# A hybrid DeltaNet/gMLP layer on one core: gate rows loaded earlier, o scaled and turned in another order, and a last tile that ends in fewer steps

## The chip, the core and the metric

The kernel runs on one core of one Trainium2 chip. The metric is device time in microseconds (us) of one execution, as the median of several runs. A profiled execution gives a trace: every instruction with its engine, its line in the kernel, its start and length.

The engines are TensorE (PE; its weight loads are listed as PEld), VectorE (DVE), ScalarE (ACT), GpSimd (POOL) and SyncE (SP), which here only issues DMAs. Each engine works through its own instructions in order, so an instruction that waits holds up everything behind it on its engine.

## The reference

One layer of a diffusion backbone, on 128 context tokens (`x_prompt`) and 2048 latent tokens (`x_sample`), model width 1024:

```python
h = modulated rmsnorm(x)                       # shift, scale, gate from c or, for the context, c_ctx
proj = h @ w_in                                # q, k, v, gate, a/b, u, vg
o_a = gated DeltaNet, forward + backward scan, 4 heads x 128, chunks of 64
o_a = rmsnorm(o_a, o_norm) * silu(gate)
o_b = gelu(u) * (w_spatial @ layernorm(gelu(vg)) + b_spatial)
x = x + gate1 * (concat(o_a, o_b) @ w_out)
h = modulated rmsnorm(x)
x = x + gate2 * (relu(h @ w_ff1) ** 2 @ w_ff2)
y = rmsnorm(x, norm_final)
```

The scan solves, for each chunk of 64 tokens, a triangular system and carries a 128 x 128 state per head from chunk to chunk. The outputs are y for both sequences and the context's two final states.

## The kernel before, in words

The 2176 tokens are 17 tiles of 128 (tile 0 is the context), `NT = 17`. The program has three stages: the head (modulation, input projections and convolution), the scan, and the MLP.

**Scan.** A unit is one tile in one direction: two units for the context, 16 forward, 16 backward. The triangular systems of two units are solved together (a pair), by doubling: `level(w)` for w = 2, 4, 8, 16, 32 makes a product into PSUM (L1173), DVE copies it under a mask into a kept matrix, P2 to P32 in this text (L1176, `copy_predicated`), and PE then takes P as an operand (L1187 and L1193). So at each level PE needs a DVE instruction that needs PE. The rest of a unit is `prep` (KK, QK: L1026, L1036), `values` and `scan` (vt L1054, S L1085, o L1108).

**Output steps.** For the context and in the backward scan, `o_steps` finishes a tile. `norm` loads ob (the gMLP half), squares o on ACT and makes 1/rms per head with a power on POOL. `scaled` multiplies that factor (L1398) and then, head by head, o by it and by the gate (four instructions at L1400). `trans(half)` turns half 0 (o) or half 1 (ob) on PE (L1413), makes a high part on ACT (oH, L1417) and a low part on DVE (oL, L1418), and, in half 0, asks for the two halves of x (L1409). `proj(n, k0)` multiplies with w_out: four steps for each of two column halves n, in groups of three matmuls, `mm3` (L220 high x high, L221, L222 with the low parts). Its last step multiplies the PSUM sum by the gate row (L1437, `tmp`), adds x (L1438) and stores (L1440). For the latent tiles the gate rows, `ga1`, are loaded once. For the context tile each row is loaded there, by `wrow` (L213), into one of the 49 buffers of 128 x 512 that `wp` has for weights, rows and activations alike; a load into such a buffer is issued by SP once the earlier user has let go.

**Order.** Each step goes into a list with a time, in units of the scan: `at(time, step, kind)`; `spread` puts a list of steps evenly in a span. `o_steps` gives its first four steps parts 0 to 1 of a window (`p3[4]` to `p3[5]`; for the context 0.4 units from `NT + 0.9`). The list is sorted by time and emitted. A scheduler then orders the instructions of each engine by a timeline of its own, so that a step moved in the list also moves others.

**MLP.** Seven Strassen-like products go over pairs of latent tiles; `todo` is the list of (product, pair, quarter). `outcome` adds a product's PSUM sum into accumulators. When a tile is whole, `final` makes its end: times the gate row, plus x, squares with a sum, 1/rms over both halves (`rsqrt_cols`: DVE at L177, POOL's power at L178), times 1/rms and norm_final (L1879), stores (L1880). `half_out` does one half; the other half is done as soon as its sum is there. The last entry of `todo` is the last sum of the last tile, with accumulator y[0].

Of the kernel before, what the change touches and what calls it, by code (L numbers as in the profile page):

```python
# [8 lines left out]
F32 = mybir.dt.float32  # L9
# [4 lines left out]
AF = mybir.ActivationFunctionType  # L14
ALU = mybir.AluOpType
# [3 lines left out]
P = 128  # L19
D = 1024  # L20
KT = D // P
# [3 lines left out]
H = 4  # L25
EPS = 1e-6
# [36 lines left out]
def hybrid_step(  # L63
# [7 lines left out]
    V, A, G, T = nc.vector, nc.scalar, nc.gpsimd, nc.tensor  # L71
    load = nc.sync.dma_start
    store = nc.sync.dma_start
# [4 lines left out]
    def yrow(t):  # L78
        return y_prompt[0] if t == 0 else y_sample[0, (t - 1) * P : t * P, :]

    def cond(t):
        return 0 if t == 0 else 1
# [9 lines left out]
    mod_d = dp.tile([2, 6 * D], F32, name="mod_d")  # L92
# [117 lines left out]
    def wrow(row):  # L210

        t = w512("row")
        load(out=t, in_=row.to_broadcast([P, 512]))  # L213
        return t
# [66 lines left out]
    with ExitStack() as ph:  # L281
# [103 lines left out]
        ps = pt()  # L385
# [541 lines left out]
    with ExitStack() as ph:  # L927
# [448 lines left out]
        def o_steps(du):  # L1376
            t = du["t"]
            out = []
            u = {}

            def norm():
                du["ob"] = w512("ob")
                load(out=du["ob"], in_=ob_d[t * P : (t + 1) * P, :])
                o, ga = du["o"], du["ga"]
                ss = smp.tile([P, 4], F32, tag="oss", name="oss")
                junk = fp.tile([P, P], BF16, tag="junk", name="junk", bufs=1)
                for h in range(H):
                    A.activation(junk, o[:, h, :], AF.Square, accum_out=ss[:, h : h + 1])
                r2 = smp.tile([P, 4], F32, tag="r2", name="r2")
                rr = smp.tile([P, 4], F32, tag="rr", name="rr")  # L1390
                V.tensor_tensor(out=r2, in0=rq[:, t, :], in1=rq[:, t, :], op=ALU.mult)
                V.tensor_tensor(out=r2, in0=r2, in1=ss, op=ALU.mult)
                rsqrt_cols(rr, r2, 4, 1.0 / P, EPS)
                u["rr"] = rr

            def scaled():
                o, ga, rr = du["o"], du["ga"], u["rr"]
                V.scalar_tensor_tensor(out=rr, in0=rr, scalar=0.5, in1=rq[:, t, :], op0=ALU.mult, op1=ALU.mult)  # L1398
                for h in range(H):
                    V.scalar_tensor_tensor(out=o[:, h, :], in0=o[:, h, :], scalar=rr[:, h : h + 1],  # L1400
                                           in1=ga[:, h * P : (h + 1) * P], op0=ALU.mult, op1=ALU.mult)

            def trans(half):
                def f():
                    if half == 0:
                        u["H"], u["L"] = [], []
                        u["x"] = [w512("x"), w512("x")]
                        for n in range(2):
                            load(out=u["x"][n], in_=xrow(t)[:, n * 512 : (n + 1) * 512])  # L1409
                    src = du["o"] if half == 0 else du["ob"].rearrange("p (h d) -> p h d", h=H)  # L1410
                    ps = pj().rearrange("p (h d) -> p h d", h=H)
                    for h in reversed(range(H)):
                        T.transpose(ps[:, h, :], src[:, h, :], ident)  # L1413
                    hs = hp.tile([P, 4, P], F32R, tag="h", name="oH")
                    ls = hp.tile([P, 4, P], F32R, tag="h", name="oL")
                    scale = 0.5 if half else vec[:, 68:69]
                    A.activation(hs, ps, AF.Copy, scale=scale)  # L1417
                    V.scalar_tensor_tensor(out=ls, in0=ps, scalar=scale, in1=f32(hs), op0=ALU.mult, op1=ALU.subtract)  # L1418
                    u["H"] += [hs[:, i, :] for i in range(4)]
                    u["L"] += [ls[:, i, :] for i in range(4)]  # L1420
                return f

            def proj(n, k0):
                def f():
                    if k0 == 0:
                        u["ps"] = pj()
                    for k in (k0, k0 + 1):
                        mm3(u["ps"], [(u["H"][k], u["L"][k]) + WO[n][k]], first=k == 0,
                            last=k == KT - 1)
                    if k0 == KT - 2:  # L1430
                        sl = slice(n * 512, (n + 1) * 512)
                        tmp = fp.tile([P, 512], F32, tag="ug" if n else "vg", name="tmp")
                        ga = ga1[n]
                        if cond(t) == 0:
                            ga = wrow(mod_d[0:1, 2 * D + n * 512 : 2 * D + n * 512 + 512])
                        x = u["x"][n]
                        V.tensor_tensor(out=tmp, in0=u["ps"], in1=ga, op=ALU.mult)  # L1437
                        V.tensor_tensor(out=x, in0=x, in1=tmp, op=ALU.add)  # L1438
                        du["x2"] = u["x"]
                        store(out=x2_d[t * P : (t + 1) * P, sl], in_=x)  # L1440
                return f

            for n in range(2):
                for k0 in range(0, KT, 2):
                    out.append(proj(n, k0))
            return [(0.0, norm, "fill"), (0.45, scaled, None), (0.7, trans(0), "fill"), (0.95, trans(1), "fill")], out

        def swap_right():
            right.close()
# [143 lines left out]
    def add(out, a, b, op=ALU.add):  # L1593
        V.tensor_tensor(out=out, in0=a, in1=b, op=op)  # L1594
# [158 lines left out]
    y0 = {}  # L1753
# [23 lines left out]
    def fetch(src, name="r2"):  # L1777
        t = w512(name)
        load(out=t, in_=src)
        return t  # L1780
# [79 lines left out]
    def half_out(y, n, x, ga, ss):  # L1860

        add(y[n], y[n], ga[n], ALU.mult)
        add(y[n], y[n], x[n])
        A.activation(x[n], y[n], AF.Square, accum_out=ss[:, n : n + 1])

    def final(t, y):

        ga = gate_rows(0) if t == 0 else rows["ga"]
        x = [fetch(x2_d[t * P : (t + 1) * P, n * 512 : n * 512 + 512], "x") for n in range(2)]
        ss = smp.tile([P, 2], F32, tag="ss2", name="ss2")  # L1870
        half_out(y, 1, x, ga, ss)

        def rest():
            half_out(y, 0, x, ga, ss)
            r = smp.tile([P, 1], F32, tag="r", name="r")
            add(ss[:, 0:1], ss[:, 0:1], ss[:, 1:2])
            rsqrt_cols(r, ss[:, 0:1], 1, 1.0 / D, EPS)
            for n in range(2):
                V.scalar_tensor_tensor(out=y[n], in0=y[n], scalar=r, in1=rows["nf"][n], op0=ALU.mult, op1=ALU.mult)  # L1879
                store(out=yrow(t)[:, n * 512 : n * 512 + 512], in_=y[n])  # L1880

        return rest
# [134 lines left out]
    for m, (n, i, u, q) in enumerate(todo):  # L2017
        us = products[n][1]
        s_next(m + AHEAD + 2, True)
        s_next(m + AHEAD, False)  # L2020
        if n == 5 and u == 0 and q == 0:
            rows["ga"] = gate_rows(1)
            rows["nf"] = row512(norm_final.unsqueeze(0))
        if q == 0:
            ps = bank()
            if i == 4:
                rest = final(pairs[u][1], [acc["v", u], acc["q", u]])
            elif i == 2:
                rest = final(0, [y0[0], y0[1]]) if u == 8 else final(pairs[u][0], [acc["x", u], acc["u", u]])
        h, lo = sops.pop(m)  # L2030
        mm3(ps, [(h[:, kp, :], lo[:, kp, :], t[:, 0, :], t[:, 1, :])
                 for kp, t in enumerate(tiles[n][4 * q : 4 * q + 4])], first=q == 0, last=q == 3)
        if m == 1:
            for t in final_turn:
                t.turn()
        if q == 3:
            outcome(i, u, ps)
            if i in (4, 2):
                rest()
        mm = m - m0[n]  # L2040
        if i == 1 and mm <= 24 and mm % 3 == 0:
            sums(1, *kept.pop("sum"))
            if mm < 24:
                kept["sum"] = (mm // 3 + 8, sums_load(1, mm // 3 + 8))
        if i in (5, 6) and mm <= 24:
            if mm % 3 == 0 and mm:
                sums(i, mm // 3 * 2 - 1, loaded)
            if mm < 24 and mm % 3 < 2:
                loaded = sums_load(i, mm // 3 * 2 + mm % 3)
                if mm % 3 == 0:  # L2050
                    early = loaded
                else:
                    sums(i, mm // 3 * 2, early)
        if u == us[-2]:
            t_next(n + 1, q)
        elif u == us[-1] and q < 3:
            for k in range(4 * q + 4, 4 * q + 8):
                t_next(n + 1, k)
# [47 lines left out]
```

## Time and profile before

| | |
|---|---|
| median of 3 runs | 2584.34 us (2582.85 to 2585.54) |
| profiled execution | 2586.25 us |
| its span, first to last instruction | 2584.5 us |
| granted PE clock, mean | 0.997 of full speed |
| PE busy | 2544.6 us, 98% |
| DVE busy | 1785.2 us, 69% |
| ACT busy | 1193.5 us, 46% |
| head | 0 to 462 us, PE busy 450.29 |
| forward scan | 462 to 880 us, PE busy 412.04 |
| context's end and first backward units | 880 to 945 us, PE busy 56.86 |
| rest of the backward scan | 945 to 1240 us, PE busy 289.31 |
| MLP | 1240 to 2576 us, PE busy all through |
| after the last matmul | 2576 to 2584.5 us |

How to read it: a row of a timeline has the start, the length, the engine, the line in the kernel, the operation, output <- inputs, shapes and a count; in brackets the idle time of the engine just ahead of it and the instruction that ended it. Rows with a count above one are several instructions in a row. `PE pd L1187 <- DVE P L1176` in the list of waits reads: PE waited at L1187, which writes pd, for DVE's instruction at L1176, which wrote P. The granted clock is the share of full speed at which the chip let PE run.

### The profile page before, as it was taken

How to read it: one execution, taken by the hardware profiler on the slowest of the kernel's cores; microseconds unless marked ns; L12 is line 12 of the kernel's file. 1: busy time of each engine (PE TensorE's matmuls, PEld its weight loads, DVE VectorE, ACT ScalarE, POOL GpSimd, SP SyncE). 2: the span in 40 equal slices, each digit the busy share in tenths (PEclk: the TensorE clock that was granted, in tenths of full speed). 3: DMA queues.
4: the chain of work that ended last, by engine and by line, in shares of the span. 5: the costliest groups of instructions: out<-in, count | busy, mean ns of one | idle time of the engine just before them, and what ended most of it. 6: DMA issues, size and time to landing. Idle time of an engine off the chain costs nothing.

```text
span 2584.5 us, 43725 instructions
## 1 busy us (share of the span) xinstructions
PE 2544.6 (98%) x15296; PEld 2135.4 (83%) x15296; DVE 1785.2 (69%) x3524; ACT 1193.5 (46%) x2758; POOL 296.7 (11%) x512
## 2 busy tenths in 40 slices
PE   8999999999999999999999999999999999999998
PEld 4899999788888778788888888888888888888887
DVE  5776746667667778896588787677785445685874
ACT  3755545554545556763254553333343333243441
POOL 3112112222222222231000000000000000000000
PEclk9999999999999999999999999999999999999999
DMA  8876637755555757996678788545599778786773
GB/s 285 286 233 199 190 128 224 241 162 169 172 168 173 220 185 240 294 309 219 250 227 238 226 277 295 153 136 160 165 299 317 275 257 295 248 258 213 231 251 105
DMA packets 533859, 579.77 MB, mean 224 GB/s; under 512 B 35500, under 2 KB 366684, under 8 KB 530054
## 3 DMA queue, kind: packets, MB, share of 16 engines
q1 hardware_dynamic: 533638, 576.98, 70.0%
q8 instruction: 120, 1.97, 0.3%
q14 instruction: 101, 0.83, 0.1%
HBM read 397.62 MB, written 179.22 MB: 223 GB/s over the span
## 4 chain that ended last, share of the span: by engine, by line
PE 56%; DVE 1%; issue 1%; POOL 0%; DMA 0%; ACT 0%; DVEq 0%; POOLq 0%; ACTq 0%
PE f L220 17%; PE f L221 17%; PE f L222 17%; PE pj L220 1%; PE pj L222 1%; PE pj L221 1%; PE f L856 0%; PE pd L992 0%; PE pd L1096 0%; PE pd L1060 0%; PE pd L1097 0%; DVE o L1400 0%; PE pm L1413 0%; DVE vt L1054 0%; PE f L270 0%
## 5 line engine op out<-in xcount | busy, mean ns | idle before, releaser
L220 PE MATMUL f<-hop,zH 128*128 128x512 f32 x960 | 373.2, 389 | 0.0
L222 PE MATMUL f<-hop,zL 128*128 128x512 f32 x960 | 373.1, 389 | 0.0
L221 PE MATMUL f<-hop,zH 128*128 128x512 f32 x960 | 373.1, 389 | 0.0
L220 PE MATMUL f<-hop,wH 128*128 128x512 f32 x896 | 351.4, 393 | 0.0
L221 PE MATMUL f<-hop,wH 128*128 128x512 f32 x896 | 348.9, 390 | 0.0
L222 PE MATMUL f<-hop,wL 128*128 128x512 f32 x896 | 344.3, 390 | 0.0
L1600 ACT CAST zH<-zraw 128x512 fp32r<-128x512 f32 x240 | 146.7, 620 | 292.3 <-DMA zraw<-s_d 95.9
L1594 DVE TENSOR_TENSOR zL<-zraw,zH 128x512 fp32r<-128x512 f32 x240 | 162.6, 688 | 78.2 <-ACT zH L1600 65.8
L222 PEld LDWEIGHTS f<-hop,zL 128*128 128x128 f32 x960 | 180.2, 188 | 37.4
L221 PEld LDWEIGHTS f<-hop,zH 128*128 128x128 f32 x960 | 180.2, 188 | 37.3
L220 PEld LDWEIGHTS f<-hop,zH 128*128 128x128 f32 x960 | 180.2, 188 | 37.3
L222 PEld LDWEIGHTS f<-hop,wL 128*128 128x128 f32 x896 | 168.2, 188 | 35.7
L220 PEld LDWEIGHTS f<-hop,wH 128*128 128x128 f32 x896 | 168.5, 188 | 34.0 <-issue 0.9
L221 PEld LDWEIGHTS f<-hop,wH 128*128 128x128 f32 x896 | 168.5, 188 | 32.1
L222 PE MATMUL pj<-kH,wL 128*128 128x386 f32 (+2 forms) x568 | 190.5, 335 | 0.0
L220 PE MATMUL pj<-kH,wH 128*128 128x386 f32 (+2 forms) x568 | 189.2, 336 | 0.6 <-DVE kH L487 0.3
L221 PE MATMUL pj<-kL,wH 128*128 128x386 f32 (+2 forms) x568 | 189.3, 333 | 0.0
L178 POOL TENSOR_TENSOR r<-rsq,nhalf 128x1 f32<-128x1 f32 (+1 forms) x38 | 22.9, 603 | 1352.7 <-DVE rsq L177 1352.7
L1747 ACT CAST wH<-s 128x512 fp32r<-128x512 f32 x96 | 58.8, 620 | 173.8 <-DVE s L1594 160.6
L537 DVE SCALAR_TENSOR_TENSOR cv<-pj,vec,cv 128x384 f32<-128x384 f32 (+2 forms) x164 | 87.3, 540 | 56.1 <-ACT cv L534 54.8
L220 PEld LDWEIGHTS pj<-kH,wH 128*128 128x128 f32 x568 | 107.1, 189 | 5.2 <-issue 4.7
L221 PEld LDWEIGHTS pj<-kL,wH 128*128 128x128 f32 x568 | 107.4, 189 | 0.6
(408 smaller groups left out, 5720.1 us busy)
## 6 DMA issues: line engine op xcount, KB each, us to landing
zraw<-z_d SPq DMA_DIRECT2D x212, 256.0 KB
raw<-in_w_ff_dram SPq DMA_DIRECT2D x128, 256.0 KB
hop<-hop_d SPq DMA_DIRECT2D x28, 1024.0 KB
z_d<-c SPq DMA_DIRECT2D x96, 256.0 KB
zraw<-s_d SPq DMA_DIRECT2D x96, 256.0 KB
raw<-in_w_mod_dram SPq DMA_DIRECT2D x80, 256.0 KB
r<-in_w_ff_dram SPq DMA_DIRECT2D x80, 256.0 KB
s_d<-s SPq DMA_DIRECT2D x64, 256.0 KB
```

What stands on the lines that cost most here:

```text
L178: G.tensor_tensor(out=out, in0=t[:np_, :n], in1=nhalf[:np_, :n], op=ALU.pow)
L220: T.matmul(ps, lh, rh, start=first and i == 0, stop=False, skip_group_check=more)
L221: T.matmul(ps, lh, rl, start=False, stop=False, skip_group_check=more)
L222: T.matmul(ps, ll, rh, start=False, stop=last and i == n - 1, skip_group_check=more)
L537: V.scalar_tensor_tensor(out=cv[:, o : o + m], in0=ps[:, s + sh : s + sh + m], scalar=convw[:, w, j : j + 1], in1=cv[:, o : o + m], op0=AL ...
L1594: V.tensor_tensor(out=out, in0=a, in1=b, op=op)
L1600: A.copy(h, src)
L1747: A.copy(h, s2)
```

## The change

The order below is that of the program's instructions on one engine. It has no times.

1. The context tile's two gate rows are loaded in `trans`, ahead of x, and no longer in the last step of `proj`.
2. `scaled` is split: the factor at part 0.42 and the four multiplications at 0.52 (both were at 0.45).
3. `trans(1)`, ob, comes first, at 0.7, and `trans(0)`, o, second, at 0.9 (they were at 0.95 and 0.7). The lists of high and low parts are filled by index, so that `proj` uses them in the same order. The loads of x go with the one that is first.
4. The last tile has an end of its own, `final_end`: y[0] times the gate row and plus x, y[1] times norm_final, and y[1]'s share of the mean are made ahead of the last sum. Behind the last sum come the sum times the gate row, one addition, the squares, one small DVE instruction, POOL's power, and then ACT scales y[1] while DVE scales y[0]. `outcome` is not called for the last sum.

In the changed program lines are renumbered: L1400 is L1403, L1409 is L1414, L1413 is L1418, L1418 is L1423, L1437 is L1440, L1438 is L1441, L1594 is L1598.

On DVE, around the copy of P16 of a pair of backward units (P16 and P32 are the kept matrices, o the tile that is finished, opL and y belong to the MLP's first operands), before:

```order
L875 TENSOR_TENSOR opL_13488<-ev_13356,opH_13487 128x512
L1400 SCALAR_TENSOR_TENSOR o_13376<-o_13376,rr_13457,ga_13152 128x128 x4
L1176 COPY_PREDICATED P16_5735<-om16_189,pd_13477 128x32x16
L875 TENSOR_TENSOR opL_13494<-ev_13396,opH_13493 128x512
L1437 TENSOR_TENSOR tmp_13512<-pm_13378,row_11527 128x512
L1026 SCALAR_TENSOR_TENSOR KK_13319<-KK_13319,nbeta_193,gr_13317 128x128 x4
L1438 TENSOR_TENSOR x_13223<-x_13223,tmp_13512 128x512
L1036 TENSOR_TENSOR QK_13365<-QK_13365,gr_13317 128x512
L1176 COPY_PREDICATED P32_5736<-om32_190,pd_13585 128x16x32
L1418 SCALAR_TENSOR_TENSOR oL_13582<-pm_13576,vec_199,oH_13581 128x512
```

The same place in the changed program:

```order
L875 TENSOR_TENSOR opL_13488<-ev_13356,opH_13487 128x512
L1176 COPY_PREDICATED P16_5735<-om16_189,pd_13477 128x32x16
L875 TENSOR_TENSOR opL_13494<-ev_13396,opH_13493 128x512
L1440 TENSOR_TENSOR tmp_13512<-pm_13378,row_11527 128x512
L1403 SCALAR_TENSOR_TENSOR o_13376<-o_13376,rr_13457,ga_13152 128x128 x4
L1026 SCALAR_TENSOR_TENSOR KK_13319<-KK_13319,nbeta_193,gr_13317 128x128 x4
L1441 TENSOR_TENSOR x_13223<-x_13223,tmp_13512 128x512
L1036 TENSOR_TENSOR QK_13365<-QK_13365,gr_13317 128x512
L1176 COPY_PREDICATED P32_5736<-om32_190,pd_13585 128x16x32
L1423 SCALAR_TENSOR_TENSOR oL_13582<-pm_13576,oH_13581 128x512
```

The four multiplications of o moved from ahead of P16's copy to behind it, and still stand ahead of P32's copy; the low part that follows P32 is now ob's.

On DVE while the context tile is finished (o is already the first backward tile's, row is the gate row, wL a low part of a weight, gr and KK belong to the next units), from the values vt to P32's copy, before:

```order
L1054 SCALAR_TENSOR_TENSOR vt_11823<-pd_12163,neg2_196,vt_11823 128x128 x4
L1400 SCALAR_TENSOR_TENSOR o_12088<-o_12088,rr_12181,ga_11814 128x128 x4
L1176 COPY_PREDICATED P16_5735<-om16_189,pd_12219 128x32x16
L1026 SCALAR_TENSOR_TENSOR KK_12012<-KK_12012,nbeta_193,gr_12010 128x128 x4
L1036 TENSOR_TENSOR QK_12065<-QK_12065,gr_12010 128x512
L192 TENSOR_TENSOR wL_12214<-raw_12018,wH_12213 128x512
L1437 TENSOR_TENSOR tmp_12207<-pm_11997,row_12208 128x512
L1176 COPY_PREDICATED P32_5736<-om32_190,pd_12312 128x16x32
```

The same place in the changed program:

```order
L1054 SCALAR_TENSOR_TENSOR vt_11823<-pd_12167,neg2_196,vt_11823 128x128 x4
L1440 TENSOR_TENSOR tmp_12211<-pm_12001,row_11871 128x512
L1176 COPY_PREDICATED P16_5735<-om16_189,pd_12221 128x32x16
L1441 TENSOR_TENSOR x_11875<-x_11875,tmp_12211 128x512
L1403 SCALAR_TENSOR_TENSOR o_12092<-o_12092,rr_12185,ga_11814 128x128 x4
L1026 SCALAR_TENSOR_TENSOR KK_12016<-KK_12016,nbeta_193,gr_12014 128x128 x4
L1036 TENSOR_TENSOR QK_12069<-QK_12069,gr_12014 128x512
L192 TENSOR_TENSOR wL_12216<-raw_12022,wH_12215 128x512
L1176 COPY_PREDICATED P32_5736<-om32_190,pd_12314 128x16x32
```

The product with the row went from behind the weight's low part to ahead of P16's copy, x's sum and the four multiplications to behind it.

On PE the first rows that differ are at the context tile too: its ob was turned just ahead of P2's use (L1187), and is now turned four groups of `mm3` sooner. Between P16 and P32 of the same pair, where o and ob are those of the first backward tile, stood before:

```order
L1060 MATMUL pd_12278<-vt_11823,T1_11787 128x128 x4
L1413 MATMUL pm_12293<-ident_173,o_12088 128x128 x4
L220 MATMUL pj_12238<-wH_12090,oH_11880 128x512
L221 MATMUL pj_12238<-wL_12091,oH_11880 128x512
L222 MATMUL pj_12238<-wH_12090,oL_11881 128x512
```

And in the changed program:

```order
L1060 MATMUL pd_12280<-vt_11823,T1_11787 128x128 x4
L220 MATMUL pj_12241<-wH_12094,oH_11916 128x512
L221 MATMUL pj_12241<-wL_12095,oH_11916 128x512
L222 MATMUL pj_12241<-wH_12094,oL_11917 128x512
L220 MATMUL pj_12241<-wH_12129,oH_11916 128x512
L221 MATMUL pj_12241<-wL_12130,oH_11916 128x512
L222 MATMUL pj_12241<-wH_12129,oL_11917 128x512
L1418 MATMUL pm_12295<-ident_173,ob_12176 128x128 x4
```

The turning that stood here was o's; ob's comes first now, behind the two groups of w_out, and o's follows the product for P32 (L1173). L1097's last matmul of the first backward tile moved behind four groups of `mm3`. SP issues the two rows (L213) just ahead of the two loads of x; before, it issued x, x and then `ga1`'s row there.

```diff
+            def factors():
+                rr = u["rr"]
+                V.scalar_tensor_tensor(out=rr, in0=rr, scalar=0.5, in1=rq[:, t, :], op0=ALU.mult, op1=ALU.mult)
+
             def scaled():
                 o, ga, rr = du["o"], du["ga"], u["rr"]
-                V.scalar_tensor_tensor(out=rr, in0=rr, scalar=0.5, in1=rq[:, t, :], op0=ALU.mult, op1=ALU.mult)
                 for h in range(H):
...
             def trans(half):
                 def f():
-                    if half == 0:
-                        u["H"], u["L"] = [], []
+                    if half:
+                        u["H"], u["L"] = [None] * KT, [None] * KT
+                        if cond(t) == 0:
+                            u["rows"] = [wrow(mod_d[0:1, 2 * D + n * 512 : 2 * D + n * 512 + 512]) for n in range(2)]
                         u["x"] = [w512("x"), w512("x")]
...
-                    u["H"] += [hs[:, i, :] for i in range(4)]
-                    u["L"] += [ls[:, i, :] for i in range(4)]
+                    for i in range(4):
+                        u["H"][half * 4 + i], u["L"][half * 4 + i] = hs[:, i, :], ls[:, i, :]
...
-                        ga = ga1[n]
-                        if cond(t) == 0:
-                            ga = wrow(mod_d[0:1, 2 * D + n * 512 : 2 * D + n * 512 + 512])
+                        ga = u["rows"][n] if cond(t) == 0 else ga1[n]
...
-            return [(0.0, norm, "fill"), (0.45, scaled, None), (0.7, trans(0), "fill"), (0.95, trans(1), "fill")], out
+            return [(0.0, norm, "fill"), (0.42, factors, None), (0.52, scaled, None), (0.7, trans(1), "fill"),
+                    (0.9, trans(0), "fill")], out
...
+    def final_end(t, y):
+
+        x = [fetch(x2_d[t * P : (t + 1) * P, n * 512 : n * 512 + 512], "x") for n in range(2)]
+        ss = smp.tile([P, 2], F32, tag="ss2", name="ss2")
+        half_out(y, 1, x, rows["ga"], ss)
+        V.tensor_scalar(out=ss[:, 1:2], in0=ss[:, 1:2], scalar1=1.0 / D, scalar2=EPS, op0=ALU.mult, op1=ALU.add)
+        add(y[1], y[1], rows["nf"][1], ALU.mult)
+        add(y[0], y[0], rows["ga"][0], ALU.mult)
+        add(y[0], y[0], x[0])
+
+        def rest(ps):
+            add(x[0], ps, rows["ga"][0], ALU.mult)
+            add(y[0], y[0], x[0])
+            A.activation(x[0], y[0], AF.Square, accum_out=ss[:, 0:1])
+            r = smp.tile([P, 1], F32, tag="r", name="r")
+            V.scalar_tensor_tensor(out=ss[:, 0:1], in0=ss[:, 0:1], scalar=1.0 / D, in1=ss[:, 1:2], op0=ALU.mult,
+                                   op1=ALU.add)
+            G.tensor_tensor(out=r, in0=ss[:, 0:1], in1=nhalf[:, 0:1], op=ALU.pow)
+            A.activation(y[1], y[1], AF.Copy, scale=r)
+            V.scalar_tensor_tensor(out=y[0], in0=y[0], scalar=r, in1=rows["nf"][0], op0=ALU.mult, op1=ALU.mult)
+            for n in range(2):
+                store(out=yrow(t)[:, n * 512 : n * 512 + 512], in_=y[n])
+
+        return rest
...
-                rest = final(0, [y0[0], y0[1]]) if u == 8 else final(pairs[u][0], [acc["x", u], acc["u", u]])
+                rest = (final(0, [y0[0], y0[1]]) if u == 8 else
+                        (final_end if u == us[-1] else final)(pairs[u][0], [acc["x", u], acc["u", u]]))
...
-        if q == 3:
+        if q == 3 and m == len(todo) - 1:
+            rest(ps)
+        elif q == 3:
             outcome(i, u, ps)
```

## The prediction

> **What bounds the kernel now.** First the time by stages (columns: window, its length, then busy time and number of instructions of PE, PEld, DVE, ACT, POOL, the granted PE clock, DMA share, GB/s).
>
> ```profile
> 880.00:945.00 65.00, 56.86 (x466) 47.02 (x465) 52.65 (x133) 33.58 (x81) 15.73 (x17) 0.95 0.70 221
> 945.00:1240.00 295.00, 289.31 (x2473) 240.15 (x2472) 233.22 (x502) 177.64 (x473) 71.57 (x77) 1.00 0.78 248
> 2060.00:2576.00 516.00, 516.00 (x2277) 427.13 (x2275) 326.58 (x539) 179.87 (x334) 10.53 (x16) 1.00 0.73 237
> 2576.00:2584.50 8.50, 0.06 (x1) 0.00 (x0) 3.81 (x7) 0.72 (x2) 0.54 (x1) 0.63 0.16 62
> ```
>
> TensorE (PE) is the bound: in the MLP it never stops, so only three things can shorten the program: PE's stops in the scan, time at a lower PE clock, and the 8.5 us after the last matmul. The change adds and removes no matmul. Where PE stops is in PE's waits from 880 to 1245 us (total, times, longest):
>
> ```profile
> PE pd L1187 <- DVE P L1176: 6.1, 7, 1.4
> PE pm L1413 <- DVE tmp L1437: 5.5, 1, 5.5
> PE pj L222 <- DVE oL L1418: 0.3, 1, 0.3
> ```
>
> These are the stops that the edits aim at, besides the tail. The profiled execution took 2586.25 us with a span of 2584.5, so 1.75 lie outside the span; it stands 1.91 above the median of 2584.34. I assume that both these differences stay, and subtract the sum from either.
>
> **Context tile: the gate rows.** PE, DVE and SP around the one long stop, one timeline of each:
>
> ```profile
> 895.22 0.40 PE L1187 MATMUL pd<-P,X 128*128 128x64 f16 x8
> ...
> 916.56 0.39 PE L1187 MATMUL pd<-P,X 128*128 128x64 f16 x8 [0.38 <-DVE P L1176]
> ...
> 919.83 0.41 PE L1173 MATMUL pd<-Y,AH 128*128 128x64 f16 x8
> 925.74 1.11 PE L1413 MATMUL pm<-ident,ob 128*128 128x128 f32 x4 [5.50 <-DVE tmp L1437]
> ```
>
> ```profile
> 894.43 0.73 DVE L1176 CAST_PREDICATED P<-om,pd 128x512 f16<-128x512 uint16 x1
> ...
> 898.45 0.69 DVE L1418 SCALAR_TENSOR_TENSOR oL<-pj,oH 128x512 fp32r<-128x512 f32 x1
> ...
> 914.78 1.13 DVE L1400 SCALAR_TENSOR_TENSOR o<-o,rr,ga 128x128 f32<-128x128 f32 x4
> ...
> 924.99 0.69 DVE L1437 TENSOR_TENSOR tmp<-pm,row 128x512 f32<-128x512 f32 x1 [5.79 <-DMA row<-mod_d]
> ```
>
> ```profile
> 888.46 0.81 SPq L1409 DMA_DIRECT2D x<-in_x_prompt_dram  x2
> ...
> 919.67 0.43 SPq L213 DMA_DIRECT2D row<-mod_d  x1
> ```
>
> SP issues the gate row at 919.67, DVE can use it at 924.99, 5.3 us later. The program asks for it only where the product is written. DVE works in order; P's copy is queued behind, and PE, which needs the PSUM buffer that DVE's product empties, stands for 5.50. In the changed program the two rows are issued with the x loads, just ahead of them, which now stand at 888.46: 36 us ahead of the use instead of 5.3. So the 5.50 go. The first product's DVE instruction now lies ahead of P16 in place of the four L1400 (0.69 instead of 1.13 and its issue), so the 0.38 at 916.56 goes too.
>
> The stop has an aftermath, seen in the granted clock in short windows:
>
> ```profile
> 922.30:923.30 1.00, 0.00 (x0) 0.00 (x0) 0.00 (x0) 0.00 (x0) 0.00 (x0) 0.74 0.93 166
> ...
> 929.00:929.60 0.60, 0.60 (x4) 0.50 (x3) 0.60 (x2) 0.60 (x2) 0.00 (x0) 0.50 0.15 51
> 929.60:930.20 0.60, 0.60 (x7) 0.60 (x7) 0.34 (x1) 0.60 (x2) 0.00 (x0) 1.00 0.00 0
> ```
>
> A mean of 0.74 in the window from 922.3 is half speed from about 922.8 on, 2.5 us after PE's last matmul ended (919.83 + 0.41), and full speed is back at 929.6. From 925.74 to 929.6 PE worked 3.86 us at half speed, which at full speed is 1.93: another 1.9 to win, if no stop of that length is left. [...] I keep 1.9 from the rows.
>
> What is given back: the context's ob is now turned sooner, so its oL (0.69, the row at 898.45) comes ahead of P2's copy on DVE. That copy ended at 895.16 and PE came at 895.22, so it had 0.06 to spare: a new wait of 0.6. At P32, DVE had done all that stands ahead of it but the row's product by 924.99 − 5.79 = 919.2; it now has that product (0.69) and x's sum (the same size) on top of it, so the copy (0.7) runs from about 920.6 to 921.3. PE has one turning left between L1173, which ended at 920.24, and P32; it takes under half of the 1.11 that it took at half clock at 925.74, so PE comes at 920.7: a wait of 0.6, bounds 0 and 1.2. The sum L1108 for o comes later, since its last product L1097 now stands behind four groups of three matmuls; I take that as hidden, because the L1400 that need o now stand behind P16 and x's sum, and if it isn't, P32 comes later by as much, which the lower bound holds. Sum for the context tile: 5.50 + 0.38 + 1.93 − 0.6 − 0.6 = 6.6 us. Bounds: 7.8 with no new wait, and 4 if both new waits are twice as long and three quarters of the clock's part stay.
>
> On SP the rows stand ahead of x, the next WO load, gr, ga1's row and vt; should a buffer come late, these wait with it. Each issue takes SP some 0.4 (the rows at 888.46 and 919.67), no other load shows up among PE's waits in this stage, and so I put nothing for it here, and its failure among the rivals.
>
> **Backward scan: o scaled behind P16.** DVE, then PE, around one P16:
>
> ```profile
> 1006.01 1.14 DVE L1400 SCALAR_TENSOR_TENSOR o<-o,rr,ga 128x128 f32<-128x128 f32 x4
> 1007.06 0.69 DVE L1176 CAST_PREDICATED P<-om,pd 128x512 f16<-128x512 uint16 x1
> ...
> 1011.50 0.69 DVE L1176 CAST_PREDICATED P<-om,pd 128x512 f16<-128x512 uint16 x1 [0.30 <-PE pd L1173]
> ```
>
> ```profile
> 1004.58 0.41 PE L1173 MATMUL pd<-Y,AH 128*128 128x64 f16 x8
> 1007.80 0.39 PE L1187 MATMUL pd<-P,X 128*128 128x64 f16 x8 [1.35 <-DVE P L1176]
> ...
> 1013.16 0.41 PE L1187 MATMUL pd<-P,X 128*128 128x64 f16 x8
> ...
> 1052.02 0.39 PE L1187 MATMUL pd<-P,X 128*128 128x64 f16 x8 [1.36 <-DVE P L1176]
> ...
> 1096.22 0.39 PE L1187 MATMUL pd<-P,X 128*128 128x64 f16 x8 [1.36 <-DVE P L1176]
> ...
> 1139.43 0.39 PE L1187 MATMUL pd<-P,X 128*128 128x64 f16 x8 [0.36 <-DVE P L1176]
> ...
> 1180.60 0.39 PE L1187 MATMUL pd<-P,X 128*128 128x64 f16 x8 [0.19 <-DVE P L1176]
> ```
>
> P16's product was done at 1004.99, and its copy could have started at 1006.01, where the four L1400 take 1007.06 − 1006.01 = 1.05 us first. Behind P16 they cost that wait nothing, so 1.35 falls to 0.30, three times: 3 × 1.05 = 3.15; the 0.36 and 0.19 go whole. Together 3.7. Late next would be P32's copy, which gets the same DVE work ahead of it. It started at 1011.50 after waiting 0.30 for PE; without that wait it starts at 1011.2 and ends at 1011.9, and PE arrives at 1013.16 − 1.05 = 1012.1. So 0.2 us are to spare, no more: bounds 3.7 and 0 (if each microsecond comes back at P32).
>
> Splitting off the factor (one L1398 of 0.15) moves no work onto PE's path, and turning ob first gives the oL that PE's last product waits for at the end of the scan earlier: 0.3, bounds 0 and 0.3.
>
> **The tail.** DVE, ACT, POOL and SP after the last matmul, then the DMA:
>
> ```profile
> 2576.82 0.69 DVE L1594 TENSOR_TENSOR hop<-hop,row 128x512 f32<-128x512 f32 x1
> 2577.55 0.69 DVE L1594 TENSOR_TENSOR hop<-hop,x 128x512 f32<-128x512 f32 x1
> 2578.33 0.63 ACT L1864 ACTIVATE x<-hop 128x512 f32<-128x512 f32 x1 [10.21 <-issue]
> ...
> 2579.08 0.16 DVE L1594 TENSOR_TENSOR ss<-ss 128x1 f32<-128x1 f32 x1 [0.84 <-ACT x L1864]
> 2579.27 0.15 DVE L177 TENSOR_SCALAR rsq<-ss 128x1 f32<-128x1 f32 x1
> ...
> 2580.15 0.75 DVE L1879 SCALAR_TENSOR_TENSOR hop<-hop,r,row 128x512 f32<-128x512 f32 x1 [0.72 <-POOL r L178]
> ...
> 2580.93 0.33 SPq L1880 DMA_DIRECT2D out_dram<-hop  x1
> 2581.59 0.33 SPq L1880 DMA_DIRECT2D out_dram<-acc  x1
> ```
>
> ```profile
> 2582.00:2582.50 0.50, 0.00 (x0) 0.00 (x0) 0.00 (x0) 0.00 (x0) 0.00 (x0) 0.50 1.03 377
> 2582.50:2583.00 0.50, 0.00 (x0) 0.00 (x0) 0.00 (x0) 0.00 (x0) 0.00 (x0) 0.50 1.02 393
> ```
>
> One of three sums goes (2577.55 − 2576.82 = 0.73), and two small steps become one (2579.27 − 2579.08 = 0.19): the power is ready 0.92 earlier. Then ACT's copy and DVE's product run beside each other. ACT's instruction isn't in the trace; its nearest row is the Square of 0.63 over as many elements, so the first store leaves some 0.1 before DVE's 0.75 would allow, and the second right behind it instead of 0.66 later: first store 1.0, second 1.25 earlier. The two stores fill the DMA engines (1.03, 1.02), so the end follows the first: 1.0, bounds 0.9 and 1.25. [...]
>
> **Sum:** 6.6 + 3.7 + 0.3 + 1.0 = 11.6. The profiled run would be 2586.25 − 11.6 = 2574.65, the median 2584.34 − 11.6 = 2572.7 us. The bounds give 4 + 0 + 0 + 0.9 = 4.9 and 7.8 + 3.7 + 0.3 + 1.25 = 13.1, or 2579.4 and 2571.2.
>
> **The rivals.** *DVE is next.* DVE was busy 233.22 of 295 us in the scan and has 0.2 us to spare at P32. If P32, or P2 after it, is late by what P16 gains, the 3.7 are gone: 7.9 left, 2576.4. For it: the small margin. Against: PE does not wait at 1013.16 now, and the moved work is no more than before.
>
> *The rows are late again, or something else is.* SP's queue waits for two more buffers, or the tile that comes next is late because the DMA engines lose the 5.5 us in which they worked ahead (share 0.93 in the window from 922.3). Then the stop moves instead of going: with half of the 6.6 left the sum is 8.3, with none of it 5.0, 2576.0 to 2579.3. Against: the rows have 36 us instead of 5. The clock adds to this case only where the stop left over is longer than the 2.5 us that the rows show.
>
> *DVE's order hurts each pair (slower).* The backward scan has eight pairs of units. If in each of them ob's low half, turned first, stands ahead of P2 (0.69) and L1400 makes P32 late by its whole 1.13, a pair loses 1.8 and the scan 14.6, against 7.9 won elsewhere: 2584.34 + 6.7 = 2591. It decides from 7.9 / 8 = 1.0 us a pair. Against: in the changed order ob's low half stands ahead of P2 in the context tile alone, and P32's copy has its margin.
>
> **Chances.** The forecast 0.66; DVE next 0.17; rows or loads late 0.13; order hurting each pair 0.04. 0.2% is 5.2 us, about what a measurement of this kernel can tell from no change: faster means under 2579.2. The forecast, DVE next and two thirds of the third case lie there, less a little for what isn't listed: 0.89 faster, 0.08 same, 0.03 slower. Range 2570.0 to 2579.3: the bounds, with 1.2 below for the scatter of the three runs (2582.85 to 2585.54), and the second and third case above.
>
> **What would show it.** Right: no wait of PE on tmp, a granted clock of 1.00 all through 880 to 945; PE's wait on P from 6.1 to about 3 (6.1 − 0.4 − 3.7 + 1.2: three of 0.3 stay, P2 and P32 in the context tile are new); in the tail two sums and 7.3 to 7.6 us from last matmul to end. Wrong: a new PE wait of over 1 us anywhere in 880 to 1240, on P32 or on a DMA, or a clock below 1 there.

## The result, and the profile after

The changed kernel takes 2578.39 us (median of 8 runs, 2575.55 to 2582.14), the kernel before 2584.06 us beside it (8 runs, 2582.35 to 2589.2). The ratio is 0.9977 with a 95% interval of 0.9968 to 0.9987. So it is faster by 5.7 us, half of the 11.6 that were forecast, and lies near the slow end of the forecast range (2570.0 to 2579.3).

The runs of one kernel scatter by several us, so the traces are cut into four parts at marks on PE, the same in every kernel: the first wait at L1149 after 880 us (all ahead of it is the same program in both), the first matmul of the MLP (L220, f <- hop), the end of the last matmul, and the end of the span. The first two marks of the changed kernel are these rows:

```profile
884.62 0.40 PE L1149 MATMUL pd<-ident,X 128*128 128x128 f16 x4 [0.81 <-DVE X L1141]
...
1241.89 0.39 PE L220 MATMUL f<-hop,wH 128*128 128x512 f32 x1
```

Their distance, 357.27, is called the scan in what follows. In the kernel before the same two rows are:

```profile
887.28 0.40 PE L1149 MATMUL pd<-ident,X 128*128 128x128 f16 x4 [0.82 <-DVE X L1141]
...
1249.82 0.39 PE L220 MATMUL f<-hop,wH 128*128 128x512 f32 x1
```

| us, profiled execution | before | after | difference |
|---|---|---|---|
| ahead of the first mark (same instructions) | 887.28 | 884.62 | −2.66 |
| scan | 362.54 | 357.27 | −5.27 |
| MLP | 1326.24 | 1326.57 | +0.33 |
| last matmul's end to the span's end | 8.44 | 7.54 | −0.90 |
| span | 2584.5 | 2576.0 | −8.5 |

The first row is scatter: over all the traces of this study, in which that part of the program is the same, the first mark lies between 881.5 and 887.3. The change itself gave 5.3 in the scan and 0.9 in the tail (the part after the last matmul); 10.6 and 1.0 were forecast.

The clock and PE's waits of the changed kernel in the scan, as they were shown of before:

```profile
880.00:945.00 65.00, 61.33 (x517) 50.58 (x515) 56.37 (x132) 35.58 (x87) 18.04 (x18) 1.00 0.73 230
```

```profile
PE pj L1418 <- DVE o L1403: 3.7, 3, 1.2
PE pd L1187 <- DVE P L1176: 3.5, 10, 1.1
PE pd L1149 <- DVE X L1141: 0.8, 1, 0.8
PE pm L1418 <- DMA ob<-ob_d: 0.8, 1, 0.8
```

The wait for the gate row is gone, the clock is full, and the waits on P fell from 6.1 to 3.5. The first line of the list is new: PE waits three times for the scaled o, 3.7 us in all, at the turning of o. That is what the prediction named as a sign of being wrong, a new wait of over 1 us; its signs of being right came too. Where these waits stand, and those that were forecast:

```profile
892.95 0.40 PE L1187 MATMUL pd<-P,X 128*128 128x64 f16 x8 [0.47 <-DVE P L1176]
...
917.80 0.66 PE L1418 MATMUL pm<-ident,ob 128*128 128x128 f32 x4 [0.77 <-DMA ob<-ob_d]
919.47 0.39 PE L1187 MATMUL pd<-P,X 128*128 128x64 f16 x8 [0.31 <-DVE P L1176]
...
998.06 0.39 PE L1187 MATMUL pd<-P,X 128*128 128x64 f16 x8 [0.30 <-DVE P L1176]
...
1025.96 0.66 PE L1418 MATMUL pj<-ident,o 128*128 128x128 f32 x4 [1.24 <-DVE o L1403]
...
1070.64 0.66 PE L1418 MATMUL pj<-ident,o 128*128 128x128 f32 x4 [1.25 <-DVE o L1403]
...
1115.34 0.66 PE L1418 MATMUL pj<-ident,o 128*128 128x128 f32 x4 [1.25 <-DVE o L1403]
```

892.95 and 919.47 are P2 and P32 at the context tile, 998.06 is a P16. The new waits lie some 28 us behind each P16: a pair of units finishes two tiles, and they are in the second. DVE there, from the sum o to P2's copy:

```profile
1012.33 0.67 DVE L1108 TENSOR_TENSOR o<-pd,of 128x512 f32<-128x512 f32 x1
...
1017.67 0.15 DVE L1392 TENSOR_TENSOR r<-r,oss 128x4 f32<-128x4 f32 x1
...
1021.71 0.16 DVE L1398 SCALAR_TENSOR_TENSOR rr<-rr,rq 128x4 f32<-128x4 f32 x1 [0.24 <-POOL rr L178]
1022.24 2.02 DVE L849 TENSOR_SCALAR x<-x,r 128x512 f32<-128x512 f32 x2 [0.36 <-POOL r L178]
1024.18 0.68 DVE L1441 TENSOR_TENSOR x<-x,tmp 128x512 f32<-128x512 f32 x1
1024.78 1.12 DVE L1403 SCALAR_TENSOR_TENSOR o<-o,rr,ga 128x128 f32<-128x128 f32 x4
1025.83 0.73 DVE L1176 CAST_PREDICATED P<-om,pd 128x512 f16<-128x512 uint16 x1
```

The squares' use (L1392) comes 5.3 us after o, behind the triangular part (L1242, L1251 and L1141 on DVE), and L849 and x's sum stand ahead of the scaling. In the kernel before, at the same tile, L1392 came 2.45 after o, ahead of L1251 and L1141, and the scaling was done when PE asked for it:

```profile
1021.53 0.67 DVE L1108 TENSOR_TENSOR o<-pd,of 128x512 f32<-128x512 f32 x1
...
1023.98 0.16 DVE L1392 TENSOR_TENSOR r<-r,oss 128x4 f32<-128x4 f32 x1 [0.40 <-ACT junk L1388]
...
1031.84 1.67 DVE L1400 SCALAR_TENSOR_TENSOR o<-o,rr,ga 128x128 f32<-128x128 f32 x3
```

### The profile page after: what moved, and what is told of

The parts are those of the page before. It is cut to its first block, busy times and chain, and to the rows that moved or that the text cites. A ratio compares the mean times of both kernels' runs of the same rounds, so it can differ in the third digit from the quotient of the medians.

```text
span 2576.0 us, 43707 instructions
## 1 busy us (share of the span) xinstructions
PE 2543.0 (99%) x15296; PEld 2133.9 (83%) x15296; DVE 1781.3 (69%) x3525; ACT 1193.0 (46%) x2759; POOL 315.1 (12%) x512
## 3 DMA queue, kind: packets, MB, share of 16 engines
q8 instruction: 120, 1.97, 0.3%
## 4 chain that ended last, share of the span: by engine, by line
PE 57%; DVE 1%; DMA 1%; ACT 1%; issue 0%; POOL 0%; SPq 0%; POOLq 0%; DVEq 0%; ACTq 0%
PE f L220 17%; PE f L221 17%; PE f L222 17%; PE pj L220 1%; PE pj L222 1%; PE pj L221 1%; PE pd L992 0%; PE f L856 0%; PE pd L1096 0%; PE pd L1097 0%; PE pm L1418 0%; PE pd L1060 0%; DMA vt<-vt_d 0%; DMA hop_d<-opL 0%; DMA gr<-g_d 0%
## 5 line engine op out<-in xcount | busy, mean ns | idle before, releaser
L220 PE MATMUL f<-hop,zH 128*128 128x512 f32 x960 | 373.2, 389 | 0.0
L222 PE MATMUL f<-hop,zL 128*128 128x512 f32 x960 | 373.2, 389 | 0.0
L220 PE MATMUL f<-hop,wH 128*128 128x512 f32 x896 | 351.4, 393 | 0.0
L222 PE MATMUL f<-hop,wL 128*128 128x512 f32 x896 | 344.3, 390 | 0.0
L222 PEld LDWEIGHTS f<-hop,zL 128*128 128x128 f32 x960 | 180.2, 188 | 37.3
L220 PEld LDWEIGHTS f<-hop,zH 128*128 128x128 f32 x960 | 180.2, 188 | 37.3
L1598 DVE TENSOR_TENSOR zL<-zraw,zH 128x512 fp32r<-128x512 f32 x240 | 162.4, 687 | 70.1 <-ACT zH L1604 56.1
L222 PEld LDWEIGHTS f<-hop,wL 128*128 128x128 f32 x896 | 168.2, 188 | 35.7
L220 PEld LDWEIGHTS f<-hop,wH 128*128 128x128 f32 x896 | 168.5, 188 | 34.0 <-issue 1.2
L222 PE MATMUL pj<-kH,wL 128*128 128x386 f32 (+2 forms) x568 | 190.5, 335 | 0.0
L220 PE MATMUL pj<-kH,wH 128*128 128x386 f32 (+2 forms) x568 | 189.2, 336 | 0.5 <-DVE kH L487 0.4
L220 PEld LDWEIGHTS pj<-kH,wH 128*128 128x128 f32 x568 | 107.0, 189 | 5.0 <-issue 4.6
```

The lines of the kernel that those rows point to most:

```text
L220: T.matmul(ps, lh, rh, start=first and i == 0, stop=False, skip_group_check=more)
L222: T.matmul(ps, ll, rh, start=False, stop=last and i == n - 1, skip_group_check=more)
```

## Experiments

Theory A: the order. Turning ob first together with the later scaling gives DVE an order in the second tile in which the scaled o is late; take either away and the waits go. Theory B: DVE is full. What P16 gains comes back at whichever DVE result is next late, in any order. Theory C: turning ob first makes o late by itself. "Scan" is the distance of the two marks in one profiled execution; medians are over 5 to 11 runs (e7: one), those of before 2582.8 (e1 to e8) and 2583.45 (e9, e10), over 16 to 23.

**e1, the changed kernel again.**

> The changed kernel again, beside the others on one chip. All theories: 5 to 6 us below the kernel before (ratio 0.9977), PE's waits on o (the scaling, L1403) 3.7 us in three, on P 3.5, none on the gate row.

Median 2577.14, ratio 0.9978 (0.9967 to 0.9988). Scan 358.08; waits on o 3.8 in three. So the scan of the changed kernel is 357.3 to 358.1.

**e2, o turned first again**, the rest of the change kept:

```diff
-                    if half:
+                    if not half:
...
-... (0.52, scaled, None), (0.7, trans(1), "fill"), (0.9, trans(0), "fill") ...
+... (0.52, scaled, None), (0.7, trans(0), "fill"), (0.95, trans(1), "fill") ...
```

> The changed kernel with o turned first again (0.7) and ob second (0.95); the rows, the later scaling and the new end stay. Theory A (the order: the swap together with the later scaling puts o's scaling of every second tile behind other DVE work): PE's three waits of 1.25 on o go, P16's waits stay at 0.3 each, and it is 3 to 5 us below the changed kernel, 9 to 11 below the kernel before. Theory B (DVE is full: what P16 gains comes back at whichever DVE result is next late): new waits of about 3.7 us at P32, P2 or a low part, and the time within 1.5 us of the changed kernel.

Median 2575.24, ratio 0.9969 (0.9957 to 0.9980), 1.9 below e1, where theory A said 3 to 5. The two intervals overlap, so the medians alone don't tell e2 from e1; the traces do. Scan 354.07: 3.2 and 4.0 shorter than the two of the changed kernel. Its waits, largest first:

```profile
PE pd L1187 <- DVE P L1176: 2.4, 6, 1.1
PE pd L1224 <- ACT R L1215: 1.0, 3, 0.3
PE pj L221 <- DVE wL L192: 0.8, 1, 0.8
PE pd L1149 <- DVE X L1141: 0.8, 1, 0.8
PE pm L1418 <- DVE o L1403: 0.6, 1, 0.6
```

And DVE in the second tile:

```profile
1013.70 0.15 DVE L1392 TENSOR_TENSOR r<-r,oss 128x4 f32<-128x4 f32 x1
...
1018.72 0.15 DVE L1398 SCALAR_TENSOR_TENSOR rr<-rr,rq 128x4 f32<-128x4 f32 x1
1020.59 0.34 DVE L1403 SCALAR_TENSOR_TENSOR o<-o,rr,ga 128x128 f32<-128x128 f32 x1
1021.46 1.67 DVE L1403 SCALAR_TENSOR_TENSOR o<-o,rr,ga 128x128 f32<-128x128 f32 x3
```

The three waits are gone, P16's stay at 0.3, and no new one of their size has come (the largest new ones are 0.8 on a weight's low part and 0.6 on o elsewhere): theory A, against B.

**e3, the four multiplications at 0.45 again**, ob still first:

```diff
-... (0.52, scaled, None), ...
+... (0.45, scaled, None), ...
```

> The changed kernel with the four multiplications of o at 0.45 again, where they were; factor at 0.42, rows, turning order and end stay. Theory A: PE's waits on o go (3.7) and P16's waits of 1.35 come back (3 x 1.05 + 0.5 = 3.7): within 1 us of the changed kernel. Theory B: the same waits at P16, and no wait on o either, since DVE has the same work: also within 1 us. A difference of over 2 us would speak against both.

Median 2577.86, ratio 0.9975 (0.9965 to 0.9985), scan 356.57. No wait on o; the waits on P are 8.6 in 14:

```profile
PE pd L1187 <- DVE P L1176: 8.6, 14, 1.4
```

So with ob first the later scaling traded its gain at P16 for waits on o. The swap alone does not make o late, which speaks against C.

**e4, only the gate rows** (loaded with x, where o is turned first):

```diff
+                        if cond(t) == 0:
+                            u["rows"] = [wrow(mod_d[0:1, 2 * D + n * 512 : 2 * D + n * 512 + 512]) for n in range(2)]
                         u["x"] = [w512("x"), w512("x")]
...
+                        ga = u["rows"][n] if cond(t) == 0 else ga1[n]
```

> The kernel before with nothing changed but the two gate rows, loaded with x in the turning that is first (o's). Prediction's step: the stop of 5.5 and 1.9 us of slow clock go, 6 to 7.8 us below the kernel before. Rival (the stop moves to a later load or to P32): a new wait of PE of 2 us or more in the 60 us behind it, 2 to 5 us below.

Median 2579.15, ratio 0.9983 (0.9974 to 0.9992): 3.65 below. Scan 357.40, 5.1 below the kernel before. The stop for the row and the slow clock are gone (1.00 from 880 to 945), but the load of ob, for which PE did not wait before, now comes 1.4 late, and P16 there 0.98 instead of 0.38:

```profile
PE pd L1187 <- DVE P L1176: 7.3, 11, 1.4
PE pm L1415 <- DMA ob<-ob_d: 1.4, 1, 1.4
```

By its time it lies in the rival's range (2 to 5 us below), by its waits between the two: most of the stop went, some 2 us of it moved to the next load and the next copy.

**e5, only the split and later scaling:**

```diff
-... (0.45, scaled, None), (0.7, trans(0), "fill"), (0.95, trans(1), "fill") ...
+... (0.42, factors, None), (0.52, scaled, None), (0.7, trans(0), "fill"), (0.95, trans(1), "fill") ...
```

> The kernel before with the factor at 0.42 and the four multiplications at 0.52, nothing else. Theory A (the later scaling costs nothing so long as o is turned first): the waits at P16 fall by 3.7, no wait on o of over 1 us in all, scan 3 to 4 us shorter than before (362.5 from the first unchanged wait to the MLP's first matmul). Theory B (DVE is full, the time comes back): scan at most 1.5 shorter. The stop for the gate row stays in both.

Median 2577.08, ratio 0.9976 (0.9967 to 0.9985). Scan 355.88, 6.7 shorter, more than theory A said. The waits on P are 3.0. The rest comes from the stop, which was to stay and did not:

```profile
919.37 0.39 PE L1187 MATMUL pd<-P,X 128*128 128x64 f16 x8 [0.78 <-DVE P L1176]
...
923.75 0.66 PE L1416 MATMUL pm<-ident,ob 128*128 128x128 f32 x4 [1.39 <-DVE tmp L1440]
```

The scheduler's new order puts the product with the row behind P32's copy, and ob's turning behind some 3 us of other matmuls, so PE works while the row is on its way; the stop is 1.39 and the clock stays full (1.00 from 880 to 945).

**e6, only ob first** (0.7 and 0.9, the multiplications at 0.45, rows in `proj`):

> The kernel before with ob turned first (0.7) and o second (0.9), nothing else. Theory A: no wait on o, since the scaling is still at 0.45; a new wait of 0.5 at P2 in the context tile, the last wait on a low part (0.3) gone; scan within 1 us of before, the gate row's stop stays. Theory C (the swap by itself makes o late): three waits on o of over 1 us, scan 3 to 4 longer.

Median 2582.17, ratio 0.9995 (0.9985 to 1.0004): no difference that can be measured. Scan 360.83, 1.7 shorter, a little more than expected, with the row's stop at 2.9 and a new wait of 1.3 for the load of ob. No wait on o. Theory C is out.

**e7, only the new end** (`final_end` and its call, nothing in the scan):

> The kernel before with the last tile's new end, nothing else. From the end of the last matmul to the end of the span 7.4 to 7.6 us instead of 8.4; the scan and the MLP as before.

One run, 2579.79 us: 7.54 from the last matmul's end to the end of the span, as in the changed kernel; scan 362.84, MLP 1326.24.

**e8, o's turning at 1.3 instead of 0.9**, ob still first:

> The changed kernel with o's turning at 1.3 instead of 0.9, so that PE takes P2 and what follows it first; DVE's work is the same. Theory A (o's turning stands on PE ahead of where the scaled o can be ready): the three waits of 1.25 on o go, scan 3 to 4 us shorter than the changed kernel's 357.3 to 358.1. Theory B: as much comes back elsewhere, mostly on a low part of o or at P2; scan within 1.5 us of the changed kernel's.

Median 2574.8, ratio 0.9968 (0.9955 to 0.9980). Scan 356.61, only 0.7 and 1.5 shorter. No wait on o is left; instead P2's copy, which stands on DVE behind the late scaling, is late in each of the three pairs:

```profile
1026.51 0.40 PE L1187 MATMUL pd<-P,X 128*128 128x64 f16 x8 [0.97 <-DVE P L1176]
...
1070.74 0.40 PE L1187 MATMUL pd<-P,X 128*128 128x64 f16 x8 [0.97 <-DVE P L1176]
...
1114.97 0.40 PE L1187 MATMUL pd<-P,X 128*128 128x64 f16 x8 [0.97 <-DVE P L1176]
```

2.9 of 3.7 came back, as B said. So it isn't only that PE asks for o too soon: what stands behind the scaling on DVE is late too. The scaling itself took 1.97 us here, where it took 1.12 in the changed kernel:

```profile
1023.45 1.97 DVE L1403 SCALAR_TENSOR_TENSOR o<-o,rr,ga 128x128 f32<-128x128 f32 x4
```

By its length e8 does not decide between the theories. The clock was halved for 3.4 us in this trace with PE busy all through (last section), which costs some 1.7, an estimate from those 3.4 us at a clock of 0.50; without it the scan would be some 354.9, where theory A put it. The median, over 5 runs, is as low as e2's, but its interval overlaps e1's too. Only the waits speak for B.

**e9, ob's turning at 0.6 instead of 0.7**, ob still first: the second tile's order on DVE is that of before.

> The changed kernel with ob's turning at 0.6 instead of 0.7: ob is still turned first, and o stands at the same place on PE, but DVE's order in the second tile of a pair is that of the kernel before again (the sum of squares ahead of the triangular part, two of the four multiplications ahead of the product with the gate row's), and ob's low part moves ahead of P32 and P2. Theory A' (DVE's order in the second tile makes the scaled o late, not the swap as such): no wait on o of over 0.5 us, at most 0.6 at each P2 or P32 for the low part, scan 354 to 356. Theory B (the time comes back in any order): scan within 0.8 of the changed kernel's 357.3 to 358.1.

Median 2576.43, ratio 0.9976 (0.9967 to 0.9985). Scan 357.59.

```profile
PE pd L1187 <- DVE P L1176: 5.2, 13, 1.1
PE pm L1418 <- DMA ob<-ob_d: 2.1, 2, 1.1
...
PE pm L1418 <- DVE o L1403: 0.3, 1, 0.3
```

The three waits on o are gone (one of 0.3 is left elsewhere), as A' said; the time isn't won, as B said. ob's load is now late in a second place, and P2 waits for ob's low part (0.43 and 0.66). With ob first, each order tried had late results of its own.

**e10, e2 a second time.**

> The changed kernel with o turned first, a second time. If its lead is real: scan 354.1 within 0.8, no wait on o of over 1 us, time 8 to 10 us below the kernel before (ratio 0.996 to 0.9975). If the first trace was a lucky one: scan 356 or more.

Median 2575.14, ratio 0.9968 (0.9956 to 0.9981), scan 354.99, one wait on o of 1.0. The scan is 0.9 from e2's, where 0.8 was allowed, but below the 356 of a lucky trace: without the swap it is 354.1 to 355.0, with it 356.6 to 358.1 in the five traces that have the swap and the row loads. So the lead in the scan is real, some 3 us on average against the two traces of the changed kernel. In the medians this version is 8 us below the kernel before and some 2 below the changed one, the latter with intervals that overlap.

## Why the prediction was half right

**The gate rows: right, a term of 6.6 that comes to 6.3 by the rows of the trace.** The stop (5.50), the wait at P16 (0.38) and the slow clock (1.93) went. P2 came 0.47 late (0.6 forecast) and P32 0.31 (0.6). Not forecast was the load of ob, 0.77 late, the second rival in a small form. Each of two edits brings it by itself: it is 1.40 late with the rows alone (e4) and 1.29 with the swap alone (e6). 7.81 − 0.47 − 0.31 − 0.77 = 6.26. That this term can be had by itself was too simple, though: e4 gives 5.1 in the scan, e5 without any change to the loads 6.7, and both together without the swap (e2, e10) 8.5 and 7.6. The scan of the kernel before is 362.5 and, in e7, 362.8. Nor do the rows add up quite to the scan: 6.26 here, 3.70 at P16, the 3.74 lost at o and 0.3 at L222 make 6.5; new small waits on P and R take 0.8 of it, and the scan measured 5.27. PE's idle time between the marks fell by 4.38 and its busy time by 0.89, less than the clock's 1.93; the 0.4 left over stay open.

**P16: right at its place, wrong in the sum.** The three waits fell to 0.30, to the hundredth, and the two small ones went. "Late next would be P32's copy", the prediction put it, and priced its margin. This step failed: P32 held, and the 3.7 came back as 3.74 at the turning of o in the pair's second tile, which the prediction did not look at. Its two pieces of DVE's order were from the first tile of a pair and from the context; the second tile's order, in which L1392 moved behind the triangular part, was not read. e2 and e3 show that it takes both edits, the later scaling and the swap. How the order makes o late is shown only in part. In all three pairs POOL's power and L849 take 1.04 and 1.14 us longer than before (2.06 and 2.02 against 1.02 and 0.88, last section); what makes them longer is not shown. At the lengths of before, o would be ready some 1.7 earlier (DVE's two stops for POOL, 0.24 and 0.36, and the 1.14), more than the 1.25 that PE waits: an estimate from the rows, and no run tests it. Why the scheduler chose the order can't be seen in a trace.

**Turning ob first: wrong.** For the backward scan the prediction counted it as a gain of 0.3, for the last low part, and at no cost. The 0.3 came (the wait at L222 is gone). But beside the later scaling the swap costs some 3 us of the scan, as e2 and e10 against e1 show; alone it costs nothing that can be measured (e6).

**The tail: right.** 0.90 for 1.0. The stores' rows in the changed kernel:

```profile
2572.39 0.33 SPq L1891 DMA_DIRECT2D out_dram<-acc  x1
2572.81 0.38 SPq L1891 DMA_DIRECT2D out_dram<-hop  x1
```

ACT's copy took 0.72, not 0.63, so the first store left no sooner than DVE's product would have let it. From the first store to the end of the span it is 3.6 us in both kernels (2580.93 to 2584.5, 2572.39 to 2576.0), from the last one 2.9 and 3.2. The first store came 0.94 earlier after the last matmul, the last one 1.18 and the end 0.90: the end moved with the first store, as was forecast from the DMA's share (1.03 and 1.02 before; 1.02 and 0.99 from 2573.5 to 2574.5 in the changed kernel).

**The rivals.** What happened is nearest to "DVE is next", which gave 2576.4: P16's gain was spent, but on o and not on P32. The rival in which each pair is hurt had the right place, the order of each pair, with 1.25 instead of 1.8 a pair, and in three pairs instead of eight. That the time lies in the range is partly luck: the range was widened for P16's gain coming back at P32 and for late loads, and the gain came back at o.

## What to carry to other kernels

Where a scheduler sets the order, an edit made for one tile moves the others too: read the new order at every kind of tile in the loop, not only where the stall was. If an instruction is moved behind a wait, the next consumer of its own result is the first candidate for the new stall, ahead of whatever follows on the queue. And try each part of a change alone and left out: here the swap, harmless alone, cost 3 us of the scan beside the later scaling, and the scan without it was shorter than with the whole change.

## What the runs showed of the hardware

**The slow clock.** The half-speed stretch in the kernel before began at 922.77 and ended at 929.60:

```profile
922.70:922.80 0.10, 0.00 (x0) 0.00 (x0) 0.00 (x0) 0.00 (x0) 0.00 (x0) 0.85 0.96 205
929.50:929.65 0.15, 0.15 (x3) 0.15 (x2) 0.15 (x1) 0.15 (x1) 0.00 (x0) 0.67 0.00 0
```

(0.85 in a window of 0.1 is half speed for the last 0.03; 0.67 in 0.15 is half speed for the first 0.1.) That is 6.83 us. In e6 and e7 it is 6.83 too (918.89 to 925.72 and 916.99 to 923.82), in e8 3.41, from 919.58 to 923.00:

```profile
916.16:919.57 3.41, 1.49 (x29) 1.38 (x30) 2.18 (x4) 1.59 (x5) 3.41 (x4) 1.00 0.83 278
...
919.50:919.60 0.10, 0.10 (x5) 0.10 (x2) 0.10 (x1) 0.10 (x2) 0.10 (x1) 0.91 1.01 389
919.60:922.90 3.30, 3.30 (x14) 2.81 (x14) 3.04 (x5) 3.30 (x8) 0.08 (x1) 0.50 0.63 204
922.90:923.10 0.20, 0.20 (x3) 0.20 (x3) 0.00 (x0) 0.05 (x1) 0.00 (x0) 0.76 1.00 389
```

The prediction took 2.5 us for the point from which a stop costs clock; it is no such point. The clock fell 2.53 us after the end of PE's last matmul in the kernel before and 2.55 in e7, but 1.00 in e6, where that matmul ended at 917.89 and the stop was 2.94:

```profile
918.80:918.95 0.15, 0.00 (x0) 0.00 (x0) 0.00 (x0) 0.15 (x1) 0.00 (x0) 0.79 0.68 177
...
925.60:925.80 0.20, 0.20 (x3) 0.20 (x3) 0.00 (x0) 0.00 (x0) 0.00 (x0) 0.71 0.59 174
```

In e8 PE was busy for 1.49 of the 3.41 us ahead of the slow stretch, with two stops of 1.15 and 0.78, and the clock was halved while PE was at work again, from 918.98 on. In e4 a stop of 1.40 left the clock at full (1.00 in each microsecond from 913 to 919), in e5 one of 1.39 (1.00 from 920 to 925). The length of a single stop doesn't tell these traces apart, and what sets the clock they don't show.

**Longer instructions on DVE and POOL.** In the changed kernel's second tile two L849 took 2.02 us (the row is shown above), where they took 0.88 before, and POOL's power there 2.06 where it took 1.02. The power in the changed kernel, then both in the kernel before:

```profile
1019.62 2.06 POOL L178 TENSOR_TENSOR rr<-rsq,nhalf 128x4 f32<-128x4 f32 x1 [6.72 <-DVE rsq L177]
...
1024.90 1.02 POOL L178 TENSOR_TENSOR rr<-rsq,nhalf 128x4 f32<-128x4 f32 x1 [4.50 <-DVE rsq L177]
1027.28 0.88 DVE L849 TENSOR_SCALAR x<-x,r 128x512 f32<-128x512 f32 x2
```

During the power DVE was busy for 1.85 of the 2.06 us in the changed kernel, and for 0.63 of the 1.02 in the kernel before; during the two L849 POOL was busy for 1.73 of the 2.02 us, and for none of the 0.88 before. The other two pairs agree with these times to 0.01. In e8 the four multiplications took 1.97, in the changed kernel 1.12. What made these instructions longer, no run here tests. The power and L849 stand ahead of the scaled o, so what they took longer makes it later: with DVE's two stops by some 1.7, the estimate given at P16, where PE waits 1.25.
